# Contrast adjustment of 48 images: rows of 64 KB in six tiles and three buffers, where there were rows of 32 KB in twelve tiles and six buffers

## The chip, the cores and the metric

The kernel runs on one core of a Trainium2 chip. The metric is the device time of one execution, in microseconds (us); the median of three executions of the kernel before is 238.84 us (238.72 to 239.09). The engines have short names in the profile: PE (TensorE, matrix multiplication), DVE (VectorE), ACT (ScalarE), POOL (GpSimd) and SP (SyncE, which here only issues DMAs). A DMA moves data between the device's main memory (HBM) and the on-chip buffer (128 partitions); 16 DMA engines do the moving for this core.

## What is computed

```python
# x: 16 x 3 x 512 x 512 float32, factor = 1.5
def reference(x, factor):
    mean = np.mean(x, axis=(2, 3), keepdims=True)
    return np.clip(mean + factor * (x - mean), 0, 1).astype(np.float32)
```

Each of the 48 images (512 x 512 values, 1 MB) has a mean of its own. The output pixel is `factor * x + (1 - factor) * mean`, cut to 0 to 1. 50.33 MB are read and 50.33 MB written, each byte once.

## The kernel before, in words

The input is seen as one flat array and cut into rows of `ROW` = 8,192 values (32 KB). A tile is 128 consecutive rows, one for each partition, 4 MB; there are 12 tiles, and since 32 rows make an image, four images to a tile. The tiles live in `ring`, six buffers of 128 x 8,192 values; tile t lies in buffer t mod 6, and everything is done in place there.

For each tile:

- `load` (L82) issues a DMA on SP's queue from HBM into the buffer. Tiles 2 and 3, and 4 and 5, are loaded by one DMA each.
- `add` sums each partition's row. ACT copies the row onto itself and accumulates its sum (L96). For tile 0 alone, DVE sums the first 4,352 columns (L91) while ACT does the other 3,840. A matmul with the constant matrix `blockw` (L100) then adds the partitions of one image, multiplies by (1 - factor) / pixels and leaves in every partition the shift of its image, in the column t of the PSUM tile `bias`. Where there are two partial sums, two matmuls accumulate.
- `clip` is two DVE passes: multiply by the factor and add the shift (L104), then the maximum with 0 and the minimum with 1 (L112).
- `store` (L85) issues a DMA from the buffer to HBM. It is issued by ACT, so it stands in ACT's instruction order between the sums.

Nothing is scheduled by a planner: `manual_schedule` leaves each engine's instructions in the order in which the program writes them, and the framework adds the semaphore waits. Loads 0 to 5 are issued at the start. The clip and the store of tile 0 go in three pieces of columns (`FIRST`: 0 to 1,024, to 3,072, to 8,192), that is in rows of 4, 8 and 20 KB. In the loop, tile t is clipped, the next tile is added, and tile t is stored; for tiles 1 and 3 the store stands ahead of the next add. The load of tile t + 5 is written into the buffer of tile t - 1, so SP waits for that store to have landed.

Of the kernel before, what the change touches and what calls it, by code (L numbers as in the profile page):

```python
# [1 line left out]

# [4 lines left out]


P = 128  # L10
ROW = 8192
BUFS = 6
FIRST = (1024, 3072)


@with_exitstack
def kernel(
    ctx: ExitStack,
    tc: tile.TileContext,
    x: bass.AP,  # L20
    factor: float,
    out: bass.AP,
):

    nc = tc.nc
    f32 = mybir.dt.float32
    Alu = mybir.AluOpType
    Act = mybir.ActivationFunctionType  # L30

    B, C, H, W = x.shape
    n_img, n_pix = B * C, H * W
    ppi = n_pix // ROW
    per_tile = P // ppi
    n_tiles = n_img // per_tile
    assert ppi * ROW == n_pix and per_tile * n_tiles == n_img

    factor = float(factor)
    wconst = (1.0 - factor) / float(n_pix)  # L40

    x_f = x.rearrange("b c h w -> (b c h w)")
    out_f = out.rearrange("b c h w -> (b c h w)")

    def dram(ap, t, c0=0, c1=ROW, n=1):
        run = [[P * ROW, n]] if n > 1 else []
        return bass.AP(
            tensor=ap.tensor, offset=t * P * ROW + c0, ap=[[ROW, P], *run, [1, c1 - c0]]
        )

    consts = ctx.enter_context(tc.tile_pool(name="consts", bufs=1))
    xpool = ctx.enter_context(tc.tile_pool(name="xpool", bufs=1))
    small = ctx.enter_context(tc.tile_pool(name="small", bufs=1))
    psum = ctx.enter_context(tc.tile_pool(name="psum", bufs=1, space=bass.MemoryType.PSUM))


    sums = small.tile([P, 2 * n_tiles], f32, name="sums")
    bias = psum.tile([P, n_tiles], f32, name="bias")

    blockw = consts.tile([P, P], f32, name="blockw")  # L60
    blocks = blockw.rearrange("p (a b) -> p a b", b=ppi)
    nc.gpsimd.memset(blockw, wconst)  # L62
    for base, step in ((0, -ppi), (ppi - 1, ppi)):
        nc.gpsimd.affine_select(  # L64
            out=blocks,
            in_=blocks,
            compare_op=Alu.is_ge,
            fill=0.0,
            base=base,
            pattern=[[step, per_tile], [0, ppi]],  # L70
            channel_multiplier=1 if step < 0 else -1,
        )


    ring = xpool.tile([P, BUFS, ROW], f32, name="ring")

    def slots(t, n=1, c0=0, c1=ROW):
        k = t % BUFS
        return ring[:, k, c0:c1] if n == 1 else ring[:, k : k + n, :]

    def load(t, n=1):
        nc.sync.dma_start(out=slots(t, n), in_=dram(x_f, t, n=n))  # L82

    def store(t, c0=0, c1=ROW):
        nc.scalar.dma_start(out=dram(out_f, t, c0, c1), in_=slots(t, 1, c0, c1))  # L85

    def add(t, c0=0):
        own = sums[:, 2 * t : 2 * t + 2]
        parts = []
        if c0:  # L90
            nc.vector.tensor_reduce(  # L91
                out=own[:, 0:1], in_=slots(t, 1, 0, c0), axis=mybir.AxisListType.X, op=Alu.add
            )
            parts.append(own[:, 0:1])
        part = slots(t, 1, c0)
        nc.scalar.activation(out=part, in_=part, func=Act.Copy, accum_out=own[:, 1:2])  # L96
        parts.insert(0, own[:, 1:2])
        shift = bias[:, t : t + 1]
        for k, part in enumerate(parts):
            nc.tensor.matmul(shift, blockw, part, start=k == 0, stop=k == len(parts) - 1)  # L100

    def clip(t, c0=0, c1=ROW):
        part = slots(t, 1, c0, c1)
        nc.vector.tensor_scalar(  # L104
            out=part,
            in0=part,
            scalar1=factor,
            scalar2=bias[:, t : t + 1],
            op0=Alu.mult,
            op1=Alu.add,  # L110
        )
        nc.vector.tensor_scalar(  # L112
            out=part, in0=part, scalar1=0.0, scalar2=1.0, op0=Alu.max, op1=Alu.min
        )

    with tc.manual_schedule():
        load(0)
        load(1)
        load(2, 2)
        load(4, 2)  # L120
        add(0, 4352)
        for c0, c1 in zip((0, *FIRST), (*FIRST, ROW)):
            clip(0, c0, c1)
            store(0, c0, c1)
        add(1)
        for t in range(1, n_tiles):
            clip(t)
            if t in (1, 3):
                store(t)
            if t + 1 < n_tiles:  # L130
                add(t + 1)
            if t not in (1, 3):
                store(t)
            if t + BUFS - 1 < n_tiles:
                load(t + BUFS - 1)


# [1 line left out]
_INS = ['x', 'factor']  # L139
_OUTS = [((16, 3, 512, 512), 'float32')]  # L140

_NUMBERS = {'factor': 1.5}


# [26 lines left out]
```

## Time and profile before

| what | value |
|---|---|
| median of three executions | 238.84 us (238.72 to 239.09) |
| the profiled execution, its own time | 238.72 us |
| span in the profile, first to last instruction | 237.0 us |
| DVE, ACT, PE busy | 112.1, 82.9, 7.6 us |
| DMA issues | 10 loads, 14 stores |
| HBM read and written | 50.33 MB and 50.33 MB, 425 GB/s over the span |
| issue to landing, first load (4 MB) | 12.28 us, from 0.80 |
| last store | issued at 210.65, landing 25.5 us later |

The span is less than the execution's time because it counts from the first to the last instruction of the program. "Busy" leaves out issuing of DMAs and waiting. In the DMA part of the page a queue's line gives its packets, the megabytes moved, and the time that its packets took as a share of 16 engines over the span; q1 is SP's queue (loads), q10 is ACT's (stores). In a table of stretches the last two columns are the share of the 16 DMA engines that was busy and the GB/s that they moved; packets are counted in the stretch in which they stand, so a short stretch can show a share a little over 1. In the timeline a line has the start, the duration, the engine, the line of the code, the operation with its output and input, and in brackets the idle time ahead of it and what ended that.

### The profile page before, as it was taken

The numbers are of one execution on the slowest core, as the hardware profiler recorded it, in microseconds if no ns is written. First come the engines' busy times: TensorE is split into PE (matmuls) and PEld (weight loads), VectorE is DVE, ScalarE is ACT, GpSimd is POOL, SyncE is SP. The second block draws the span as 40 slices with busy tenths as digits, with TensorE's granted clock in tenths as the row PEclk, the third lists the DMA queues.
The fourth block names the chain that finished last, engine by engine and source line by source line (L and its number), as shares of the span: only waits on it lengthen the run. The fifth ranks groups of instructions, "written<-read, shape, count | busy, mean of one in ns | idle before, by whom it ended". The sixth has DMA issues, their size and how long they took to land.

```text
span 237.0 us, 211 instructions
## 1 busy us (share of the span) xinstructions
PE 7.6 (3%) x26; PEld 6.5 (3%) x26; DVE 112.1 (47%) x29; ACT 82.9 (35%) x25; POOL 1.0 (0%) x7
## 2 busy tenths in 40 slices
PE   0000000000000000000000000000000000000000
PEld 0000000000000000000000000000000000000000
DVE  0078708609990059979209407704902920950000
ACT  2050190299100894650380091083056029000000
POOL 1000000000000000000000000000000000000000
DMA  7999998999999999999999999999999999999996
GB/s 265 442 442 442 398 459 383 441 428 435 465 426 404 409 442 442 442 442 442 442 426 431 404 420 442 442 442 442 442 442 426 415 398 442 442 442 442 442 442 265
DMA packets 3712, 100.66 MB, mean 425 GB/s; under 512 B 384, under 2 KB 384, under 8 KB 512
## 3 DMA queue, kind: packets, MB, share of 16 engines
q1 hardware_dynamic: 1696, 50.33, 49.6%
q10 hardware_dynamic: 2016, 50.33, 49.2%
HBM read 50.33 MB, written 50.33 MB: 425 GB/s over the span
## 4 chain that ended last, share of the span: by engine, by line
DMA 39%; DVE 25%; another core or an unknown queue 11%; ACT 9%; issue 3%; PE 1%; ACTq 1%; SPq 0%
DMA out_dram<-ring 20%; DMA ring<-in_x_dram 18%; DVE ring L104 11%; DVE ring L112 11%; ACT ring L96 9%; DVE sums L91 2%; PE bias L100 1%; ACTq L85 1%; SPq L82 0%
## 5 line engine op out<-in xcount | busy, mean ns | idle before, releaser
L96 ACT ACTIVATE ring<-ring 128x8192 f32<-128x8192 f32 (+1 forms) x12 | 80.7, 6724 | 117.3 <-DMA ring<-in_x_dram 95.3
L104 DVE TENSOR_SCALAR ring<-ring,bias 128x8192 f32<-128x8192 f32 (+3 forms) x14 | 54.3, 3880 | 84.9 <-PE bias L100 84.9
L112 DVE TENSOR_SCALAR ring<-ring 128x8192 f32<-128x8192 f32 (+3 forms) x14 | 53.4, 3817 | 0.5
L100 PE MATMUL bias<-sums,blockw 128*128 128x1 f32 x26 | 7.6, 361 | 194.0 <-ACT ring L96 193.5
L100 PEld LDWEIGHTS bias<-sums,blockw 128*128 128x128 f32 x26 | 6.5, 312 | 195.0 <-ACT ring L96 177.7
L91 DVE TENSOR_REDUCE sums<-ring 128x1 f32<-128x4352 f32 x1 | 4.7, 4685 | 13.1 <-DMA ring<-in_x_dram 13.1
L96 ACT ACTIVATION_READ_ACCUMULATOR ring<-ring 128x1 f32 x12 | 2.2, 186 | 0.0
L96 ACT ACT_TABLE_LOAD x1 | 1.3, 1283 | 0.8 <-PEq L152 0.8
L64 POOL TENSOR_SCALAR_AFFINE_SELECT blockw<-blockw 128x128 f32<-128x128 f32 x2 | 0.6, 311 | 0.1
L62 POOL MEMSET blockw<- 128x128 f32 x1 | 0.2, 204 | 0.3 <-POOLq L152 0.3
L152 POOL MEMSET const-uint8-127<- 128x1 uint8 x1 | 0.1, 103 | 0.0
L152 POOL MEMSET const-bfloat16-1.0<- 128x1 bf16 x1 | 0.1, 102 | 0.0
L152 POOL MEMSET const-float32-0.0<- 128x1 f32 x1 | 0.1, 98 | 0.3 <-issue 0.3
L152 POOL MEMSET const-float32-1.0<- 128x1 f32 x1 | 0.1, 98 | 0.0
## 6 DMA issues: line engine op xcount, KB each, us to landing
out_dram<-ring ACTq DMA_DIRECT2D x11, 4096.0 KB, 48.5
ring<-in_x_dram SPq DMA_DIRECT2D x8, 4096.0 KB, 31.4
ring<-in_x_dram SPq DMA_DIRECT2D x2, 8192.0 KB, 59.5
out_dram<-ring ACTq DMA_DIRECT2D x1, 2560.0 KB, 37.3
out_dram<-ring ACTq DMA_DIRECT2D x1, 1024.0 KB, 25.8
out_dram<-ring ACTq DMA_DIRECT2D x1, 512.0 KB, 16.1
```

Source lines behind the costliest of these rows:

```text
L62: nc.gpsimd.memset(blockw, wconst)
L64: nc.gpsimd.affine_select(out=blocks, in_=blocks, compare_op=Alu.is_ge, fill=0.0, base=base, pattern=[[step, per_tile], [0, ppi]], channel ...
L85: nc.scalar.dma_start(out=dram(out_f, t, c0, c1), in_=slots(t, 1, c0, c1))
L91: nc.vector.tensor_reduce(out=own[:, 0:1], in_=slots(t, 1, 0, c0), axis=mybir.AxisListType.X, op=Alu.add)
L96: nc.scalar.activation(out=part, in_=part, func=Act.Copy, accum_out=own[:, 1:2])
L100: nc.tensor.matmul(shift, blockw, part, start=k == 0, stop=k == len(parts) - 1)
L104: nc.vector.tensor_scalar(out=part, in0=part, scalar1=factor, scalar2=bias[:, t : t + 1], op0=Alu.mult, op1=Alu.add,)
L112: nc.vector.tensor_scalar(out=part, in0=part, scalar1=0.0, scalar2=1.0, op0=Alu.max, op1=Alu.min)
L152: nc = _bacc.Bacc("TRN2", target_bir_lowering=False, num_devices=1)
```

## The change

The rows become 16,384 values (64 KB), so a tile is 8 MB, eight images; there are six tiles and three buffers, as large together as the six were. Sixteen rows make an image.

- Loads 0, 1 and 2 are issued at the start, one DMA each; load t + 3 is written after store t, whose buffer it fills, and SP waits for all pieces of that store to have landed.
- Every tile's sum is shared: DVE sums the first columns (7,168 for tiles 0 and 5, 4,352 for the others) and ACT the rest (9,216 or 12,032). Every tile has two matmuls, DVE's part first.
- Tile 0 is clipped and stored in rows of 4, 12 and 48 KB; tiles 3 and 5 in two halves of 32 KB rows; tiles 1, 2 and 4 whole.
- The loop over tiles is written out. Each store stands ahead of the next tile's add on ACT, but the second half of store 3 stands behind ACT's sum of tile 4.

```diff
-ROW = 8192
-BUFS = 6
-FIRST = (1024, 3072)
+ROW = 16384
+BUFS = 3
+CUTS = {0: (1024, 4096), 3: (8192,), 5: (8192,)}
+SUMS = {0: 7168, 5: 7168}
+SUM = 4352
...
+    def pieces(t):
+        cuts = CUTS.get(t, ())
+        return list(zip((0, *cuts), (*cuts, ROW)))
...
-    def add(t, c0=0):
+    def add(t):
+        cut = SUMS.get(t, SUM)
         own = sums[:, 2 * t : 2 * t + 2]
...
+        nc.vector.tensor_reduce(
+            out=own[:, 0:1], in_=cols(t, 0, cut), axis=mybir.AxisListType.X, op=Alu.add
+        )
+        part = cols(t, cut)
         nc.scalar.activation(out=part, in_=part, func=Act.Copy, accum_out=own[:, 1:2])
...
+        nc.tensor.matmul(shift, blockw, own[:, 0:1], start=True, stop=False)
+        nc.tensor.matmul(shift, blockw, own[:, 1:2], start=False, stop=True)
...
     with tc.manual_schedule():
-        load(0)
-        load(1)
-        load(2, 2)
-        load(4, 2)
-        add(0, 4352)
-        for c0, c1 in zip((0, *FIRST), (*FIRST, ROW)):
-            clip(0, c0, c1)
-            store(0, c0, c1)
+        for t in range(BUFS):
+            load(t)
+        add(0)
+        for k in range(len(pieces(0))):
+            clip(0, k)
+            store(0, k)
+        load(3)
         add(1)
-        for t in range(1, n_tiles):
-            clip(t)
-            if t in (1, 3):
-                store(t)
-            if t + 1 < n_tiles:
-                add(t + 1)
-            if t not in (1, 3):
-                store(t)
-            if t + BUFS - 1 < n_tiles:
-                load(t + BUFS - 1)
+        clip(1, 0)
+        store(1, 0)
+        load(4)
+        add(2)
+        clip(2, 0)
+        store(2, 0)
+        load(5)
+        add(3)
+        clip(3, 0)
+        store(3, 0)
+        clip(3, 1)
+        add(4)
+        store(3, 1)
+        clip(4, 0)
+        store(4, 0)
+        add(5)
+        for k in range(len(pieces(5))):
+            clip(5, k)
+            store(5, k)
```

More of the change, by code (lines that the diff above doesn't have):

```diff
@@ L43, with dram @@
     out_f = out.rearrange("b c h w -> (b c h w)")
[L45 to L49, printed above, removed]
+    def dram(ap, t, c0=0, c1=ROW):
+        return bass.AP(tensor=ap.tensor, offset=t * P * ROW + c0, ap=[[ROW, P], [1, c1 - c0]])
     consts = ctx.enter_context(tc.tile_pool(name="consts", bufs=1))
@@ L75, with cols, load, store @@
     ring = xpool.tile([P, BUFS, ROW], f32, name="ring")
[L77 to L85, printed above, removed]
-    def add(t, c0=0):
-        own = sums[:, 2 * t : 2 * t + 2]
[L89 to L95, printed above, removed]
+    def cols(t, c0=0, c1=ROW):
+        return ring[:, t % BUFS, c0:c1]
+    def pieces(t):
+        cuts = CUTS.get(t, ())
+        return list(zip((0, *cuts), (*cuts, ROW)))
+    def load(t):
+        nc.sync.dma_start(out=cols(t), in_=dram(x_f, t))
+    def store(t, k):
+        c0, c1 = pieces(t)[k]
+        nc.scalar.dma_start(out=dram(out_f, t, c0, c1), in_=cols(t, c0, c1))
+    def add(t):
+        cut = SUMS.get(t, SUM)
+        own = sums[:, 2 * t : 2 * t + 2]
+        nc.vector.tensor_reduce(
+            out=own[:, 0:1], in_=cols(t, 0, cut), axis=mybir.AxisListType.X, op=Alu.add
+        )
+        part = cols(t, cut)
         nc.scalar.activation(out=part, in_=part, func=Act.Copy, accum_out=own[:, 1:2])
-        parts.insert(0, own[:, 1:2])
         shift = bias[:, t : t + 1]
[L99 to L103, printed above, removed]
+        nc.tensor.matmul(shift, blockw, own[:, 0:1], start=True, stop=False)
+        nc.tensor.matmul(shift, blockw, own[:, 1:2], start=False, stop=True)
+    def clip(t, k):
+        part = cols(t, *pieces(t)[k])
         nc.vector.tensor_scalar(
```

## The prediction

> **What bounds the kernel now.** I read the page first (shares of the engines, then the DMA queues), then stretches of the span with their DMA share, then the timeline. The page:
>
> ```profile
> PE 7.6 (3%) x26; PEld 6.5 (3%) x26; DVE 112.1 (47%) x29; ACT 82.9 (35%) x25; POOL 1.0 (0%) x7
> ...
> q1 hardware_dynamic: 1696, 50.33, 49.6%
> q10 hardware_dynamic: 2016, 50.33, 49.2%
> ```
>
> No compute engine is half busy. The two DMA queues (q1 the loads of SP, q10 the stores of ACT) keep the 16 DMA engines busy for 49.6 + 49.2 = 98.8% of the span. The windows show where the rest is (last columns: DMA share, GB/s):
>
> ```profile
> 0.00:1.80 1.80, 0.00 (x0) 0.00 (x0) 0.00 (x0) 1.00 (x1) 1.03 (x7) 1.00 0.00 0
> 1.80:24.00 22.20, 1.15 (x4) 1.00 (x4) 10.14 (x6) 3.78 (x3) 0.00 (x0) 1.00 1.01 425
> 24.00:78.00 54.00, 1.76 (x6) 1.50 (x6) 30.71 (x8) 21.55 (x7) 0.00 (x0) 1.00 1.00 427
> 78.00:194.00 116.00, 4.11 (x14) 3.52 (x14) 62.34 (x14) 49.58 (x15) 0.00 (x0) 1.00 1.00 434
> 194.00:236.00 42.00, 0.58 (x2) 0.50 (x2) 8.92 (x2) 6.99 (x2) 0.00 (x0) 1.00 0.98 424
> 236.00:237.00 1.00, 0.00 (x0) 0.00 (x0) 0.00 (x0) 0.00 (x0) 0.00 (x0) 1.00 0.00 0
> ```
>
> From 1.8 us to near 236 the DMA share is 1.00: there is no hole to close. So this is a sum of DMA packets, and the waits that the chain and the wait table name (ACT on loads, DVE on PE) lie beside it. The change can win only by making packets cheaper, and lose only by opening a hole or making them dearer.
>
> **What one row costs.** A packet is one row of one partition: 12 tiles x 128 rows + 10 loads x 16 small completion packets = the 1,696 of q1. Four windows hold rows of one size on q10 (23 to 36, 36 to 48.2, 48.5 to 65.5 and 196 to 237 us):
>
> ```profile
> q1 hardware_dynamic: 160, 5.24, 94.1%
> q10 hardware_dynamic: 144, 0.52, 9.9%
> ...
> q10 hardware_dynamic: 144, 1.05, 20.3%
> ...
> q10 hardware_dynamic: 144, 2.62, 35.9%
> ...
> q10 hardware_dynamic: 592, 16.78, 94.8%
> ```
>
> Share x window x 16 engines / rows, with the completion packets left in the row's price: 4 KB 0.099 x 13 x 16 / 128 = 0.161 us; 8 KB 0.309; 20 KB 0.763; 32 KB 0.948 x 41 x 16 / 512 = 1.2147. From 4 to 32 KB that is 1.054 us per 28 KB, 27.2 GB/s per engine, and 0.161 - 0.1505 = 0.010 us per row that does not depend on its size. The first window also shows how the queues share: 144 packets of q10 beside 160 of q1, one row of each in turn, whatever its size.
>
> **The change, part by part.**
>
> *Longer rows.* Loads go from 96 rows of 32 KB per engine to 48 of 64 KB. No such row stands in the trace. At the slope above it costs 1.2147 + 1.2043 = 2.419; the lower bound is the slope alone, 2.409; above, 64 KB at the 20 KB row's mean rate is 2.441, at the 4 KB row's (the poorest) 2.574. I take 2.419: four sizes lie on one line, and 32 KB is the nearest. Before, per engine: loads 96 x 1.2147 = 116.61, stores 88 x 1.2147 + 8 x (0.161 + 0.309 + 0.763) = 116.75; sum 233.36. After: loads 48 x 2.419 = 116.11; stores 24 x 2.419 (tiles 1, 2, 4) + 32 x 1.2147 (halves of 3 and 5) + 8 x (0.161 + 0.462 + 1.817) (tile 0: 4, 12, 48 KB, the last two interpolated) = 58.06 + 38.87 + 19.52 = 116.45; sum 232.56. **Difference -0.8 us.** Fewer DMA issues (24 to 16, 0.34 us each on SP and ACT) fall on sequencers that are not the bound.
>
> *Sums shared by DVE and ACT.* Every tile now has a DVE reduce of columns that ACT did before, so DVE rises from 112 to about 112 - 4.7 + 31,744 columns x 1.077 ns (the row of 4,685 ns for 4,352) = 142 us, and ACT falls. Off the path as long as stores reach q10 before the queues run dry. Six tiles and three buffers make that a real question: load 3 waits for all of store 0. The rows:
>
> ```profile
> 13.11 3.40 ACT L96 ACTIVATE ring<-ring 128x3840 f32<-128x3840 f32 x1 [11.03 <-DMA ring<-in_x_dram]
> 13.11 4.68 DVE L91 TENSOR_REDUCE sums<-ring 128x1 f32<-128x4352 f32 x1 [13.11 <-DMA ring<-in_x_dram]
> ...
> 22.34 2.88 DVE L104 TENSOR_SCALAR ring<-ring,bias 128x5120 f32<-128x5120 f32 x1
> 25.26 2.83 DVE L112 TENSOR_SCALAR ring<-ring 128x5120 f32<-128x5120 f32 x1
> 28.56 7.03 ACT L96 ACTIVATE ring<-ring 128x8192 f32<-128x8192 f32 x1 [11.96 <-DVE ring L112]
> ...
> 36.36 4.49 DVE L104 TENSOR_SCALAR ring<-ring,bias 128x8192 f32<-128x8192 f32 x1 [8.28 <-PE bias L100]
> 40.89 4.43 DVE L112 TENSOR_SCALAR ring<-ring 128x8192 f32<-128x8192 f32 x1
> ```
>
> *When the first two tiles are ready.* Load 0 lands at 13.1 now; 8 rows per engine that are 1.204 longer put it at 22.7. ACT sums 9,216 columns: (7.03 - 3.40) / 4,352 = 0.833 ns a column, so 7.9, plus 0.1 to read the sum: 30.7. DVE sums 7,168: 7.7, 30.4. The two matmul pairs (0.6 each, the second after the first): 31.6. Clip: both passes over 1,024 take 1.5 (18.48 to 19.96), and (4.49 + 4.43 - 2.88 - 2.83) / 3,072 = 1.045 ns a column beyond that, so 3,072 take 3.6 and 12,288 take 13.2: stores issued at 33.1, 36.7 and 49.9. Behind the third issue stands ACT's sum of tile 1 (12,032 columns, 10.3): 60.7, matmul 61.4, clip of 16,384 (17.5): **store 1 is issued at 78.9.** DVE's 4.7 for tile 1 runs under ACT's 10.3.
>
> *When the queues run dry without it.* The 233.36 of work land at 210.65 + 25.5 = 236.15 (issue and landing of the last store), as if it had begun at 2.8. Loads 0 to 2 and store 0 are 24 x 2.419 + 19.5 = 77.6, in whatever order they take turns: dry at 80.4. Store 1 is issued 1.5 before. From an issue to the first data: the first load is issued at 0.8 and the DMA share is 0 until 1.8, so 1.0; an upper bound is its landing, 12.28 - 8 x 1.2147 = 2.6, which holds the start-up of every engine too. I take 1.0: no hole, with 0.5 us to spare. By 2.6 it would be a hole of 1.1.
>
> *After that.* Busy until: 80.4 + store 1 and load 3 (19.4 each) = 119; store 2 comes at 78.9 + 10.7 (ACT sum, issue) + 0.7 + 17.5 = 108, so 138; load 4 when store 1 has landed (about 115), so 158; load 5 when store 2 has landed (about 153). Tile 3 lands near 124: first half clipped 20 later, at 145. Then the one new wait on ACT's queue: the second half of store 3 stands behind ACT's sum of tile 4, which waits for load 4 (about 160), so it and store 4 behind it come at 171 and 190. The work queued by then lasts (halves of store 3 and load 5 added) until 187 without, 197 with the second half: 16 and 7 to spare. Nobody but the end waits for them, since no load follows load 5. Tile 5 lands near 190; its halves are issued at 208 and 217, against queues full until 216 and 226. Nothing there opens a hole.
>
> *Sum.* Span 237.0 - 0.8 = 236.2. This execution took 238.72, 1.72 around the span, so 237.9; its time lies 0.12 under the median of the runs shown, 238.84, so **238.0**.
>
> **Rivals.**
>
> *Cut rows (no saving).* If a 64 KB row goes out as two of 32 KB, the sum is 144 x 1.2147 + 38.87 + 19.52 = 233.3 and the time 238.8. For it: nothing in the trace is over 32 KB. Against it: every row up to 32 KB is one packet.
>
> *A hole at 80 us.* By the 2.6 above, 1.1: 239.1. Every us by which store 1's data is later than 80.4 adds one. Against it: 0.5 to spare; for it: the chain to 78.9 has six extrapolated durations in a row, and a late store 1 delays load 4 too.
>
> *Dearer rows, the losing side.* The 64 KB pitch between partitions moves the 16 engines through HBM at larger distances, and rows run below the 27.2 GB/s per engine. There are 72 of them per engine; from 2.419 + 0.8 / 72 = 2.430 on the saving is gone, from 2.437 the kernel is slower by over 0.2%. At the 20 KB row's rate 1.6 are added: 239.6; at the 4 KB row's, 11: 249. For it: nothing in this trace has that pitch; against it: loads at 32 KB pitch, stores too, run on one line with the small pieces at the same pitch. The Trainium skill ("DMA: Bandwidth & Descriptors", Latency and other measured facts) speaks against large power-of-two pitches: 16 KiB rows at 512 KiB pitch gave 207 GB/s where 214 is full. By its ratio, 3.4% on 72 x 2.419, this kernel would come to 243.9; the before trace shows 434 GB/s at 32 KB pitch and cannot show 64.
>
> **How the numbers follow.** About 0.2% (0.5 us) is what a measurement of this kernel can tell from no change. Forecast 0.52, all of it faster. Cut rows 0.10, within. Hole 0.15: 0.10 within, 0.05 slower. Dearer rows 0.18 and what I have not thought of 0.05: slower. So faster 0.52, same 0.20, slower 0.28. The range: below, the slope alone (72 x 0.010 = 0.7) gives 237.3; above, it takes in the hole and the 20 KB price with a hole, 240.6, and leaves out the dearer half of the dearer rows. The forecast's own range is 237.3 to 238.4.
>
> **What would show it.** Packets: q1 864 and q10 1,440 if rows go whole (6 x 128 + 96; 10 x 128 + 160). The windows: DMA share 1.00 from 1.8 to about 235, with none below in 79 to 83. q10's windows of 64 KB rows: 2.42 a row. Timeline: store 1 issued at 78.9, the last half at 217. I am wrong if a window inside shows a share under 0.95, or a row over 2.437.

## The result

The changed kernel takes 240.64 us (median of six, 239.76 to 241.01) where the kernel before, run beside it, takes 238.98 (238.72 to 239.09): a ratio of 1.0064, interval 1.0040 to 1.0088. It is 0.6% slower; 238.0 was forecast, in a range of 237.3 to 240.6. The profiled execution took 239.79, with a span of 238.1. Other executions had spans of up to 239.3; the kernel before does not scatter like this. Here and below a ratio is one of means, not of the medians beside it, and leaves out slow executions, those more than 1.5% above the fastest of their kernel.

The page of the changed kernel, the lines that answer to those shown of before (engines, packets, the two queues):

```profile
span 238.1 us, 176 instructions
...
PE 6.7 (3%) x24; PEld 5.9 (2%) x24; DVE 139.7 (59%) x26; ACT 58.5 (25%) x13; POOL 1.1 (0%) x7
...
q1 hardware_dynamic: 864, 50.33, 49.9%
q10 hardware_dynamic: 1440, 50.33, 48.9%
```

The packets are those of whole 64 KB rows (864 and 1,440). The queues' shares already show where the time is. Share times span is the time that one engine spends on a queue's packets: q1 0.499 x 238.1 = 118.8 us where 116.1 were forecast; q10 0.489 x 238.1 = 116.4, forecast 116.45. The stores cost what was forecast, the loads 2.7 us more. In the kernel before the loads took 0.496 x 237.0 = 117.55, which is 0.9 over the 116.6 that the prediction counted for them. (A share is rounded to 0.1%, which is 0.24 us.)

The stretches of the changed kernel's span from 24 us on (the last two columns are the DMA share and GB/s):

```profile
24.00:79.00 55.00, 2.16 (x8) 1.94 (x8) 46.81 (x11) 17.02 (x4) 0.00 (x0) 1.00 1.01 433
79.00:83.00 4.00, 0.00 (x0) 0.00 (x0) 4.00 (x1) 3.91 (x1) 0.00 (x0) 1.00 0.81 352
83.00:120.00 37.00, 1.18 (x4) 1.01 (x4) 17.66 (x3) 6.41 (x2) 0.00 (x0) 1.00 1.01 423
120.00:236.00 116.00, 3.36 (x12) 2.93 (x12) 69.93 (x13) 28.62 (x6) 0.00 (x0) 1.00 1.00 434
```

The 0.81 at 79 to 83 is no hole. A packet is counted in the stretch in which it starts, and with rows of 2.4 us a stretch of 4 us can hold one start too few; the stretches on both sides are over 1. By the trace the last rows of store 0 end at 81.0 and the first of store 1 start at 80.6, with no engine idle between. Store 1 was issued in time:

```profile
33.03 17.05 ACTq L88 DMA_DIRECT2D out_dram<-ring  x3
...
78.71 0.34 ACTq L88 DMA_DIRECT2D out_dram<-ring  x1
...
107.67 0.34 ACTq L88 DMA_DIRECT2D out_dram<-ring  x1
```

That is the timeline of the changed kernel, stores 0, 1 and 2 (forecast 33.1, 78.9 and 108). The line to look at is that of 83 to 120: the engines are busy all the time (1.01), yet 423 GB/s are moved where the next line has 434. **A full DMA share says that every engine has a packet in hand, not that the packet moves at full speed.** That stretch alone lacks 11 x 37 / 434 = 0.9 us.

Here are two windows of the changed kernel's DMA view inside it, first 85.6 to 92 us:

```profile
q1 hardware_dynamic: 22, 1.44, 70.2%
q10 hardware_dynamic: 17, 1.11, 40.1%
```

Then 92 to 112 us:

```profile
q1 hardware_dynamic: 64, 4.19, 48.4%
q10 hardware_dynamic: 64, 4.19, 48.4%
```

In the second every row takes 0.484 x 20 x 16 / 64 = 2.42 us, load or store: the price that was extrapolated. In the first a store row takes 0.401 x 6.4 x 16 / 17 = 2.42, but a load row 0.702 x 6.4 x 16 / 22 = 3.27. These 22 are the first rows of load 3 on all 16 engines, and a few second ones: 0.85 x 22 / 16 = 1.2 us lost per engine. Ahead of them the load queue had been empty; load 3 was issued at 81.5, when store 0 had landed, and its first row started 4.2 us later. Between 64.4 and 85.6 us only q10 has packets:

```profile
DMA packets 257, 9.67 MB, mean 456 GB/s; under 512 B 32, under 2 KB 32, under 8 KB 32
...
q10 hardware_dynamic: 257, 9.67, 105.5%
```

The same arithmetic for the load rows beside tile 0's short stores gives 0.04 x 128 / 16 = 0.3 us lost from 36 to 57 and 0.19 x 32 / 16 = 0.4 from 57 to 63.5. The first row of every engine is stretched in both kernels. The changed kernel's window of 1.7 to 4 us, then the window of 1.7 to 2.8 of the kernel before:

```profile
q1 hardware_dynamic: 16, 1.05, 135.9%
...
q1 hardware_dynamic: 16, 0.52, 169.8%
```

These rows take 1.359 x 2.3 x 16 / 16 = 3.13 us for 2.42, and 1.698 x 1.1 x 16 / 16 = 1.87 for 1.21: 0.7 lost in each. With the start that makes 2.6 of the 2.7.

### The profile page after: what moved, and what is told of

It is laid out like the page before. It is cut to its first block, busy times and chain, and to the rows that moved or that the text cites. A ratio compares the mean times of both kernels' runs of the same rounds, so it can differ in the third digit from the quotient of the medians.

```text
span 238.1 us, 176 instructions
## 1 busy us (share of the span) xinstructions
PE 6.7 (3%) x24; PEld 5.9 (2%) x24; DVE 139.7 (59%) x26; ACT 58.5 (25%) x13; POOL 1.1 (0%) x7
## 3 DMA queue, kind: packets, MB, share of 16 engines
q10 hardware_dynamic: 1440, 50.33, 48.9%
## 4 chain that ended last, share of the span: by engine, by line
DMA 44%; DVE 36%; ACT 9%; PE 1%; issue 0%; ACTq 0%; SPq 0%
DMA ring<-in_x_dram 23%; DMA out_dram<-ring 21%; DVE ring L104 15%; DVE ring L112 15%; ACT ring L97 9%; DVE sums L93 6%; PE bias L100 1%; PE bias L99 0%; ACTq L88 0%; SPq L84 0%
## 5 line engine op out<-in xcount | busy, mean ns | idle before, releaser
L97 ACT ACTIVATE ring<-ring 128x12032 f32<-128x12032 f32 (+1 forms) x6 | 56.7, 9447 | 139.9 <-DMA ring<-in_x_dram 101.9
L104 DVE TENSOR_SCALAR ring<-ring,bias 128x8192 f32<-128x8192 f32 (+4 forms) x10 | 53.4, 5342 | 28.7 <-PE bias L100 28.7
L93 DVE TENSOR_REDUCE sums<-ring 128x1 f32<-128x4352 f32 (+1 forms) x6 | 34.0, 5662 | 49.1 <-DMA ring<-in_x_dram 49.1
L112 DVE TENSOR_SCALAR ring<-ring 128x8192 f32<-128x8192 f32 (+4 forms) x10 | 52.8, 5280 | 0.3
L99 PE MATMUL bias<-sums,blockw 128*128 128x1 f32 x12 | 3.5, 360 | 171.9 <-DVE sums L93 171.9
L100 PE MATMUL bias<-sums,blockw 128*128 128x1 f32 x12 | 3.5, 359 | 21.4 <-ACT ring L97 21.4
L97 ACT ACTIVATION_READ_ACCUMULATOR ring<-ring 128x1 f32 x6 | 1.1, 186 | 0.0
```

The source lines that it names most:

```text
L93: nc.vector.tensor_reduce(out=own[:, 0:1], in_=cols(t, 0, cut), axis=mybir.AxisListType.X, op=Alu.add)
L99: nc.tensor.matmul(shift, blockw, own[:, 0:1], start=True, stop=False)
L100: nc.tensor.matmul(shift, blockw, own[:, 1:2], start=False, stop=True)
L104: nc.vector.tensor_scalar(out=part, in0=part, scalar1=factor, scalar2=bias[:, t : t + 1], op0=Alu.mult, op1=Alu.add,)
L112: nc.vector.tensor_scalar(out=part, in0=part, scalar1=0.0, scalar2=1.0, op0=Alu.max, op1=Alu.min)
```

## The experiments

What had to be told apart: whether long rows are dear, whether a queue that runs empty and rejoins pays, or whether rows pay when the other queue's rows change in length. A queue joins when its rows start beside those of the other queue. "Lost" below is the time of a queue's rows in a window of the DMA view over their plain price (2.42 us for 64 KB, 1.21 for 32 KB), per engine.

**The changed kernel again.**

> The changed kernel as it is, a second look. Theory 1 (restart): the load queue is empty from 64 to 86 us, and the first 64 KB row of load 3 on each engine then takes about 3.6 us where every other takes 2.418; so 1.2 us per engine are lost there, in this profile too, and a profile with a span near 239.3 shows a larger loss at the same rows. Theory 2 (long rows are dear in general): the rows inside are over 2.42 all along. Expected by theory 1: median 239.8 to 241, load queue's mean row 2.47, the store queue's 2.42.

240.79 us in five executions (240.71 to 240.91), ratio 1.0078 (1.0065 to 1.0091); the profiled span is 239.0. The rows of load 3 from 85 to 94 us lost 0.9 for the 1.2 of the first profile, the load rows from 57 to 63.5 lost 1.0 for 0.4; nearly all other rows take 2.42, so long rows are not dear in general. A longer span with a smaller loss at load 3 is not what was expected. Its end shows something else. The stretches of this run:

```profile
235.00:236.00 1.00, 0.00 (x0) 0.00 (x0) 0.00 (x0) 0.00 (x0) 0.00 (x0) 1.00 1.21 524
236.00:237.00 1.00, 0.00 (x0) 0.00 (x0) 0.00 (x0) 0.00 (x0) 0.00 (x0) 1.00 0.16 66
```

A share of 1.21 in one us is 1.21 x 16 / 1.21 = 16 starts of 32 KB rows, one on each engine, and 0.16 is two: two engines still start a row after 236, when the other fourteen have their last in hand. In the first profile the sixteen starts of 235 to 236 are the last. So the higher times are those of the slowest engine: the 128 rows of a DMA are eight for each engine, and the rows left to the two late engines were not taken over by the fourteen others. By the packets' durations the rows cost 0.2 us more per engine than in the first profile, and the wait for the last engines 0.8 more. The Trainium skill says the same of another case, in an explanation that it marks as unconfirmed ("DMA: Bandwidth & Descriptors", SWDGE vs HWDGE vs iDMA): a bulk load runs at the pace of its slowest engine.

**Short rows on the load queue, to keep it from emptying.**

```diff
+    spare = consts.tile([P, 2, 128], f32, name="spare")
+    x_f_head = dram(x_f, 0, 0, 128)
...
         for t in range(BUFS):
             load(t)
+        for k in range(2):
+            nc.sync.dma_start(out=spare[:, k, :], in_=x_f_head)
```

> The changed kernel, and after load 2 two more loads of 128 rows of 512 bytes into a spare tile that nobody reads, issued at the start: 18 short turns on the load queue that keep it from running empty between load 2 and load 3. They add 0.19 MB. Theory 1 (an emptied queue pays for its restart): the first rows of load 3 take 2.42 like the others and the time falls by about 1.2 less 0.3 for the short rows, to about 239.0 where the changed kernel takes 239.8. Rival (the cost belongs to the first reads after a stretch of writes alone, whether the queue is empty or not, or to the landing of store 0): the first rows of load 3 still take about 3.6 and the time rises by 0.3.

240.31 us (239.77 to 243.10), ratio 1.0079 (1.0048 to 1.0109). The short rows were too few. The last of them start at 81.5 us, load 3 is issued at 81.9, and its rows start at 85.9: the load queue is still empty, for 4 us in place of 21. The window of 81.6 to 85.8 us has q10 alone, and then that of 85.6 to 92 us:

```profile
q10 hardware_dynamic: 16, 1.05, 57.6%
...
q1 hardware_dynamic: 23, 1.51, 60.2%
q10 hardware_dynamic: 25, 1.64, 59.0%
```

A load row is now 0.602 x 6.4 x 16 / 23 = 2.68, so 0.4 is lost for the 1.2 and 0.9 of the changed kernel's two profiles. That points to the place and to the length of the empty stretch, but rows at 116 to 136 us lose 0.3 that they did not lose before, and the time is that of the changed kernel. The forecast 239.0 was a miss, and what a queue that never empties would have done is not shown by this run.

**Load 3 in halves.**

```diff
-        load(3)
+        for c0 in (0, ROW // 2):
+            nc.sync.dma_start(
+                out=cols(3, c0, c0 + ROW // 2), in_=dram(x_f, 3, c0, c0 + ROW // 2)
+            )
```

> The changed kernel with load 3 in two halves of columns (two DMAs with rows of 32 KB). If the restart has a fixed price, the first 32 KB row of load 3 on each engine takes 1.213 + 1.2 = 2.4 and the time stays (plus 0.07 for eight more rows). If the price goes with the row's length, the first row takes about 1.8 and the time falls by 0.6.

246.32 us, ratio 1.0311 (1.0294 to 1.0328): neither of the two forecasts. The first rows of load 3 lose 0.1 and the store rows beside them 0.3 (85 to 92 us), and then the whole stretch in which the two queues hold rows of different length crawls. Its stretches:

```profile
60.00:85.00 25.00, 1.17 (x4) 1.00 (x4) 22.05 (x3) 6.37 (x3) 0.00 (x0) 1.00 1.01 433
85.00:147.00 62.00, 1.18 (x4) 1.01 (x4) 22.14 (x3) 5.81 (x3) 0.00 (x0) 1.00 1.01 403
147.00:190.00 43.00, 1.60 (x6) 1.43 (x6) 32.05 (x7) 19.39 (x4) 0.00 (x0) 1.00 0.99 427
```

Share 1.01 and 403 GB/s for 62 us. Rows on both queues are stretched, by up to about 1 us each. By the sum of the rows the edit costs 0.07 us; what else it changes is which rows meet on the engines.

**Tile 0 whole, in the changed kernel, then with one short load behind load 2 too.**

```diff
-CUTS = {0: (1024, 4096), 3: (8192,), 5: (8192,)}
+CUTS = {3: (8192,), 5: (8192,)}
```

> The changed kernel with tile 0 clipped and stored whole (no pieces of 4, 12 and 48 KB), so that up to the end of store 0 both queues hold 64 KB rows alone; store 0 is issued near 49 us while loads last until 61, so no hole. Theory 2 (rows on one queue turn dearer when the other queue's rows change in length or column, seen as 0.2 to 0.7 on the load rows at 36 to 40 and 57 to 62 us of the changed kernel's two profiles): those 0.5 to 1.1 us per engine are gone and the time falls to about 239.3 to 239.9. Theory 1 alone (only the restart of the emptied load queue pays, at 86 us): the loss at 36 to 62 does not depend on the pieces, the time stays at 239.8 to 240.8.

> The same with one load of 128 rows of 512 bytes into a spare tile behind load 2 (nine short turns that keep the load queue from emptying before load 3). If an emptied queue pays for its restart, another 0.8 us less than with whole store 0 alone, near 238.5, and no first row of load 3 over 2.6. If the price of load 3's first rows is that of a change in what the other queue holds, they still show 0.4 to 1.2 and the time is the same as without it.

241.52 us (ratio 1.0105, 1.0072 to 1.0138) and 242.02 (1.0127, 1.0077 to 1.0177). Both medians are above the changed kernel's, though the intervals overlap, and neither gain that was forecast is there. In the first, between 50.6 and 53 us, just as the first store row joins the loads:

```profile
q1 hardware_dynamic: 16, 1.05, 145.3%
```

Sixteen load rows of 1.453 x 2.4 x 16 / 16 = 3.49 us, one on each engine: 1.07 lost at once, where the pieces had cost 0.7 in the first profile of the changed kernel and 1.1 in the second. So the short pieces are not the trouble. The rows of load 3 at 86 us lose next to nothing in these two, though the load queue is empty ahead of them, from 72 to 85.6 us in the first and, behind the short rows, from 82 to 85.9 in the second: an emptied queue does not always pay where it rejoins.

**The same order of work with rows of 32 KB.**

```diff
-        nc.sync.dma_start(out=cols(t), in_=dram(x_f, t))
+        for c0 in (0, 8192):
+            nc.sync.dma_start(out=cols(t, c0, c0 + 8192), in_=dram(x_f, t, c0, c0 + 8192))
...
-        nc.scalar.dma_start(out=dram(out_f, t, c0, c1), in_=cols(t, c0, c1))
+        for c0, c1 in ((0, 8192), (8192, ROW)) if c1 - c0 == ROW else ((c0, c1),):
+            nc.scalar.dma_start(out=dram(out_f, t, c0, c1), in_=cols(t, c0, c1))
```

> The changed kernel's order of work with every load and every whole store in two DMAs of half rows, so rows are 32 KB but for tile 0's pieces (4, 12, 48). The rows themselves cost 0.65 us more per engine in sum (72 pairs at 9 ns). If long rows make the stalls, they shrink to those of the kernel before (0.4 us) and the time is near 239.3; if the stalls come from the queue that empties and from rows of unequal length, they stay, and the time is 240.5 to 241.5.

243.38 us, ratio 1.0187 (1.0170 to 1.0205), above both forecasts. Its stretches:

```profile
60.00:84.00 24.00, 0.58 (x2) 0.50 (x2) 21.70 (x3) 4.84 (x3) 0.00 (x0) 1.00 1.01 437
84.00:98.00 14.00, 1.18 (x4) 1.00 (x4) 6.59 (x2) 7.07 (x2) 0.00 (x0) 1.00 1.00 374
98.00:190.00 92.00, 2.35 (x8) 2.00 (x8) 51.37 (x10) 20.64 (x4) 0.00 (x0) 1.00 1.00 433
...
218.00:220.80 2.80, 0.00 (x0) 0.00 (x0) 2.80 (x2) 0.00 (x0) 0.00 (x0) 1.00 0.19 82
```

Load 3 joins in the second of these, and 14 us at 374 GB/s for 434 are 1.9 us. Short rows lose as well, so it is not the length of the rows that loses the time there. The last line is a hole, which the changed kernel does not have: the last tile lands at 202 us (191 there), its first half is stored at 219.9, and the store queue has run dry before that. The engines are idle for over 2 us, so the time of this run is not the price of stretched rows alone.

**The kernel before with tile 0 whole.**

```diff
-FIRST = (1024, 3072)
+FIRST = ()
```

> The kernel before with tile 0 clipped and stored whole, all rows 32 KB. Theory 2: the 0.4 us per engine by which its load rows are over 1.213 between 35 and 65 us is gone, and the time is 238.4 to 238.6 (three packets of 0.16 to 0.76 become one of 1.213, 0.1 less). Otherwise it stays at 238.9.

242.55 us, ratio 1.0147 (1.0120 to 1.0173), where 238.4 to 238.9 was expected: the pieces of 4, 8 and 20 KB in the kernel before are worth 3.6 us. The window of 29 to 31.1 us, just before its first store rows start:

```profile
q1 hardware_dynamic: 32, 1.05, 151.4%
```

Two load rows on each engine at 1.514 x 2.1 x 16 / 32 = 1.59 us in place of 1.21. After that, from 92 to 193 us, load rows lose 0.1 to 0.35 once in each round of 19.4 us, which the kernel before never does. By the packets' durations the rows take 1.8 us more per engine, of the 3.5 by which its profiled span is longer; most of the rest is the wait for the last engines, since the first is through at 236.8 us and the last at 239.3.

**Ways to soften both joins of the changed kernel.**

Load 2 in quarters of columns, rows of 16 KB:

```diff
-        nc.sync.dma_start(out=cols(t), in_=dram(x_f, t))
+        n = 4096 if t == 2 else ROW
+        for c0 in range(0, ROW, n):
+            nc.sync.dma_start(out=cols(t, c0, c0 + n), in_=dram(x_f, t, c0, c0 + n))
```

Tile 0 in rows of 4, 8, 20 and 32 KB, alone and then with the quarters:

```diff
-CUTS = {0: (1024, 4096), 3: (8192,), 5: (8192,)}
+CUTS = {0: (1024, 3072, 8192), 3: (8192,), 5: (8192,)}
```

> The changed kernel with load 2 in four quarters of columns (rows of 16 KB, 32 turns on the load queue for 8), so that the load queue still holds rows when load 3 is issued near 75 us; rows cost 0.2 us more per engine, store 2 comes 2 us later, before the queues run dry. If the stretched first rows of load 3 come from an emptied queue that joins a running store stream, they are gone (no row of load 3's first two turns over 2.5), and the time is 239.5 or less. If it is any change of row length that pays, the rows of 16 KB pay at 43 us and 64 KB ones beside the stores of tile 1 at 80 us, and the time stays at 240 to 241.

> The changed kernel with tile 0 in the pieces of the kernel before and a last half: rows of 4, 8, 20 and 32 KB (four stores for three). If the store queue's joining is paid by the step in row length (4 KB beside loads cost 0.1 to 0.2 a turn, 4 to 12 KB 0.4 to 1.0, 32 KB at once 0.76, 64 KB at once 1.1 in the runs so far), the load rows between 36 and 64 us lose 0.4 as in the kernel before, where the changed kernel lost 0.66 and 1.1; the time falls by 0.2 to 0.6, to 239.8 to 240.4. Otherwise no change.

> Both: load 2 in quarters and tile 0 in rows of 4, 8, 20 and 32 KB. If the two joins are all that the changed kernel loses to the kernel before, the sum of rows (0.5 us under it) shows at last: 238.4 to 238.8, under the kernel before. If engines that fall out of step cost on their own, 239.5 or more.

The quarters gave 251.52 us (ratio 1.0529, 1.0512 to 1.0547), the worst of all. The load queue holds rows until load 3 joins, but now the store queue runs empty: store 0 is through by 75.3 us, store 1 is issued at 78.8, and its first row starts at 83.4. The window of 75.4 to 83.3 us has loads alone; then that of 81 to 141 us:

```profile
q1 hardware_dynamic: 192, 3.41, 100.4%
...
DMA packets 391, 22.54 MB, mean 376 GB/s; under 512 B 47, under 2 KB 47, under 8 KB 47
...
q10 hardware_dynamic: 216, 13.11, 54.1%
q1 hardware_dynamic: 175, 9.44, 44.7%
```

The bytes are those of 200 store rows and 144 load rows of 64 KB: 2.60 and 2.98 us each for 2.42, on both queues, over 60 us. The finer pieces alone changed nothing (240.82, ratio 1.0075, 1.0060 to 1.0090), and the load rows beside them lost 0.9 where 0.4 was expected. Both together gave 239.44 to 243.13 in ten executions (median 241.41; ratio without the 243.13 1.0079, 1.0047 to 1.0111), in the range that was named for engines out of step. There the join of load 3 was as hoped, the rows at 85 to 92 us at 2.51; from 81 to 141 us it moved 427 GB/s, with load 2 in the same quarters. This is the end of its profiled execution:

```profile
234.00:235.00 1.00, 0.00 (x0) 0.00 (x0) 0.00 (x0) 0.00 (x0) 0.00 (x0) 1.00 1.21 524
235.00:236.00 1.00, 0.00 (x0) 0.00 (x0) 0.00 (x0) 0.00 (x0) 0.00 (x0) 1.00 0.08 33
236.00:237.00 1.00, 0.00 (x0) 0.00 (x0) 0.00 (x0) 0.00 (x0) 0.00 (x0) 1.00 0.08 33
237.00:238.00 1.00, 0.00 (x0) 0.00 (x0) 0.00 (x0) 0.00 (x0) 0.00 (x0) 1.00 0.00 0
238.00:239.00 1.00, 0.00 (x0) 0.00 (x0) 0.00 (x0) 0.00 (x0) 0.00 (x0) 1.00 0.08 33
```

At 234 to 235 sixteen rows start (1.21 x 16 / 1.21). Then one row at a time (0.08 x 16 / 1.21 = 1): a single engine still has three rows to do after all others have their last in hand. It sets the end, 3 us or so behind them.

**The emptied load queue, with 32 KB rows and the order of the kernel before.**

```diff
-BUFS = 6
+BUFS = 5
...
-        load(4, 2)
+        load(4)
```

> The kernel before with five buffers for six (load 4 alone, not 4 and 5 in one): the load queue runs empty once load 4 is in, near 58 us, until store 0 has landed. Theory 1: the first 32 KB row after that takes 1 us or so more than 1.213 on each engine, once, though the row length is that of the kernel before. If only 64 KB rows pay, it takes 1.21 to 1.3.

> The kernel before with five buffers, this time in rounds: rows of 32 KB, the order of work unchanged, one difference: the load queue runs empty at 61 us and rejoins at 66 to 68. If an emptied load queue alone costs what the changed kernel lost, the time is 240.0 to 240.8 against 238.9; if that one look was chance, 238.9 to 239.2.

240.36 us in one execution, then 240.48 in six (240.32 to 241.36): ratio 1.0065, interval 1.0051 to 1.0080. That is as large as the changed kernel's loss, with rows of 32 KB. The load queue is empty from 61 to 66 us; then its load rows from 74 to 77.5 us:

```profile
q1 hardware_dynamic: 23, 0.75, 73.2%
q10 hardware_dynamic: 16, 0.36, 23.9%
```

They take 0.732 x 3.5 x 16 / 23 = 1.78 us for 1.21. The rows that rejoin at 66 are not stretched, a miss for "the first row pays"; the loss comes 9 us later. Five buffers also make the later loads wait for other stores than six do, so the emptied queue is not the one difference. At the end, 0.23 x 16 / 1.21 = 3 rows start in a stretch in which the kernel before starts none:

```profile
235.00:236.00 1.00, 0.00 (x0) 0.00 (x0) 0.00 (x0) 0.00 (x0) 0.00 (x0) 1.00 1.14 492
236.00:237.00 1.00, 0.00 (x0) 0.00 (x0) 0.00 (x0) 0.00 (x0) 0.00 (x0) 1.00 0.23 98
```

**Five and six buffers with short rows behind the first loads.**

```diff
         load(4)
+        nc.sync.dma_start(out=spare, in_=dram(x_f, 0, 0, 128))
```

With six buffers the new line stands behind `load(4, 2)`. `spare` is a tile of 128 x 128 values that nothing reads.

> The same, and behind load 4 one load of 128 rows of 512 bytes into a spare tile (nine short turns, 0.03 us each), which keeps the load queue from emptying at 61 us. If it is the emptying that costs (the engines then take up load 5 in different turns and stay out of step), the time goes back to 239.0 to 239.4 (the short rows are 0.25). If five buffers cost for another reason (later loads), it stays at 240 or goes 0.25 above.

> The kernel before, six buffers, with the same short load behind load 5: what nine short rows cost where the load queue never empties. By their sum 0.25 us: 239.1 to 239.2. If changes of row length on a running queue push the engines out of step, 239.6 or more.

With six buffers 239.31 us, ratio 1.0015 (1.0006 to 1.0024): the short rows cost the 0.3 that their sum gives where the load queue never empties. With five buffers one execution took 239.16, as expected of a queue that does not empty, and five took 242.8 to 244.4, more than without the short rows. The profile of one of these has a hole near its end:

```profile
226.00:228.00 2.00, 0.00 (x0) 0.00 (x0) 1.62 (x1) 0.00 (x0) 0.00 (x0) 1.00 0.23 98
```

The last load lands at 210.9 us (203.5 with five buffers and no short rows), the last store is issued at 227.7, and the store queue has run dry by then: 1.8 us of idle time per engine, by the packet records. Besides, as load 5 joins at 69 to 71 us, store rows lose 0.3, though the load queue held short rows until 69. No verdict on the emptied queue follows from six executions that fall so far apart and differ by a hole.

No version beat the kernel before.

## Why the prediction was wrong, step by step

**What bounds the kernel: right.** DMA share 1.00, and nearly all of the 1.1 us between the two profiled spans lies in DMA packets.

**The price of a row: right.** 2.42 us for 64 KB (2.419 forecast), 116.4 for all stores (116.45). The rival of cut rows is out by the packet counts. The rival of dearer rows is out too, in the form in which it was put: rows at 64 KB pitch run at the slope of the short ones for most of the span, so what the Trainium skill says of large power-of-two pitches ("DMA: Bandwidth & Descriptors", Latency and other measured facts) does not reach down to 64 KB here; the 120 to 236 us of the changed kernel move 434 GB/s, as the kernel before did.

**The compute chain and the hole at 80 us: right.** Store 1 at 78.71 for 78.9, stores 0 to 2 within 0.4 us, and no hole. One wait was misread, without harm: the second half of store 3 was put at 171, behind the end of ACT's sum of tile 4, but it was issued at 162.27, as that sum began.

**The sum: this failed.** The step was "this is a sum of DMA packets ... The change can win only by making packets cheaper, and lose only by opening a hole or making them dearer", with one price for a row whatever runs beside it. The term "loads 48 x 2.419 = 116.11" measured 118.8. The lost 2.7 lie in the start (0.7), in the load rows beside the first stores (0.7) and in the first rows of load 3 (1.2), each shown above by the price per row in a window. The forecast was made by difference, so what counts is what the kernel before does not lose. It loses the 0.7 at the start and 0.4 beside its own first stores, so about 1.5 is new, most of it at load 3.

The packets' durations in the two traces add up without the rounding of the shares: per engine the loads take 118.7 us for 117.7 and the stores 116.4 for 116.7, so 0.8 more, where 0.8 less was forecast. The last 0.3 of the 1.1 between the spans lies in what the sum of durations hides: at times more than 16 packets are open, so packets of an engine overlap a little, 0.8 us per engine before and 0.5 now, with 88 packets fewer. With no row stretched the saving would by this have been 0.5 and not 0.8. The prediction's own check was there to see: 116.61 counted against 0.496 x 237 = 117.55 on the page, 0.9 us that the loads took and the sum did not hold. Its own sign of being wrong, a row over 2.437, is met by the 3.27 of load 3.

**What else is in the median.** The profile is of the shorter kind of execution (239.79), of which there were two in six; it is the second kind, up to 241.0, that took the median out of the range. In the second profile of this kernel the slowest engine ends some 1 us behind. That is shown for this one and not for each execution. That the shorter kind lies inside the range is luck: the range was widened for a hole and for dearer rows throughout, and neither is there.

**Why the load queue matters.** The empty load queue was put down as harmless ("load 3 waits for all of store 0", "dry at 80.4") because the stores keep the engines busy meanwhile. Three buffers force it: loads are dry at 64 us and rejoin at 86. The kernel before with five buffers, whose load queue empties too, loses as much (0.65%) in rows of 32 KB. That the emptying is the cause is not shown: the run that kept the five buffers' queue filled gave no verdict, an empty stretch of 4 us in place of 21 took the loss of load 3's rows from 1.2 to 0.4 and did not take the time back, and with tile 0 whole, as with five buffers, the rejoining rows lost next to nothing.

**What stays open** is what stretches a row. The stretched rows are load rows at a join in most runs, and rows of both queues in the two worst ones and in the changed order with rows of 32 KB; unequal rows on the two queues go with it in one of the two worst, equal rows of 64 KB in the other. By the packet starts in the traces, the 16 engines of the kernel before take their load rows and their store rows together from 66 us on, and lose nothing; in most others some engines load while the rest store. Being split does not lose time by itself: with five buffers about six engines do the one and ten the other from 80 to 190 us, at 434 GB/s. The losses fall where the engines come to be split, and whether that is cause or effect no run here settles. Nor did any run change where the rows that meet lie in HBM.

## What to carry to other kernels

Where two DMA queues share the engines, a full DMA share is not a floor: divide the share by the packets, window by window, and compare GB/s between stretches of equal share before calling a transfer-bound kernel a sum. Check the sum of row prices against each queue's share on the page, and look for the place of any remainder. Treat a load queue that never empties and first stores that grow by steps as things that an edit can lose: in the kernel before, five buffers for six, with a load queue that empties once, cost 0.65%, and stores that began at full length 1.5%, with no hole in either. Look at the last us of a profile too: there one late engine, or a last store issued after its queue ran dry, can cost more than all stretched rows.

## What the runs showed of the hardware that was not expected

- Load rows took 0.85 to 1.07 us longer on average where the two queues join (64 KB: 3.27 and 3.49 for 2.42), and 0.4 longer over two rows of 32 KB (1.59 for 1.21), with all engines counted busy.
- With rows of 64 KB on both queues the same kind of traffic ran at 434 GB/s in the changed kernel (120 to 236 us) and at 376 in a variant (81 to 141 us), whose edit is load 2 in quarters of columns. With the same quarters and finer first pieces it ran at 427 in the same stretch, so the quarters alone do not decide it.
- A DMA issued on an empty queue while the other queue was running had its first row 3.6 to 4.6 us later (store 0 and load 3 of the changed kernel, store 1 of the variant with quarters), where the first load of all needed 1.0.
- Engines did not even out: one of 16 ended about 3 us after the others had their last rows in hand in one profiled execution, and with five buffers nine short packets per engine, 0.25 us by their sum, were followed by times from 239.2 to 244.4, with a hole of 1.8 us in the one that was profiled.
